# A two-layer encoder on one core: attention of the second mixer moved ahead of the third and fourth gated projections, latent vectors normalized by ScalarE out of PSUM

## The chip, the core and the metric

The kernel runs on one core of a Trainium2 chip. A core has five engines that each work through their own instruction list in order: TensorE (PE in the profile), VectorE (DVE), ScalarE (ACT), GpSimd (POOL) and SyncE (SP, which only issues DMAs here). They signal each other with semaphores. The metric is the device time of one execution in microseconds (us), median of three runs.

## What is computed

Two inputs of 256 tokens by 1024 features go through the same two-layer trunk; the kernel puts them side by side as 512 tokens. Each layer is a mixer, a residual layernorm, a convolutional feed-forward (FFN) and another residual layernorm. The change lies in the second mixer:

```
h = x @ w_in                                   # 1024 -> 256 + 128 + 32 + 512 + 512
c_q, c_kv, k_r, glu_a, glu_g = split(h)
q  = rmsnorm(c_q,  gq)  @ w_uq                 # 8 heads of 64 + 32 (the 32 are rotated)
kv = rmsnorm(c_kv, gkv) @ w_ukv                # 8 heads of 64 + 64
c  = softmax((q_nope.k_nope + q_rope.rope(k_r)) * 96**-0.5) @ v
d  = glu_a * sigmoid(glu_g)                    # the gated projection, 512 channels
d  = silu(layernorm(dwconv31(d)))              # depthwise, 31 taps along the tokens
mix = concat(c, d) @ w_out
```

All matrix products of weights are done in split fp32: each operand is a rounded high part and a low remainder, and a product is three matmuls (high by high, high by low, low by high).

## The kernel before

The kernel is written as Python loops, and a scheduler of the framework then decides the order on each engine: it lists the instructions by its own estimate of when each can start, and tile pools decide when a buffer comes free. So the order in the program text is a priority and not the final order. Pools that matter here: `actp` with 30 SBUF tiles of 4 KB per partition, `wp` with 12 weight tiles, `rawp` with 4 tiles that SyncE loads weights into, and PSUM banks in `pA` (4), `pB` (2) and `pC` (2).

`wload` (L103) loads a weight block, rounds it on ScalarE (L107, the high part) and subtracts on VectorE (L109, the low part). During the down projection of the first FFN, `KEEP` (L29) lets `glu_load` prepare all four gated weight blocks ahead, in `actp` tiles called khi and klo.

The second mixer is `odd_mixer` (L521). Its parts:

- `glu(i)` (L525), i = 0 to 3: two 128-channel projections of 24 matmuls each, sigmoid on ScalarE, product on VectorE into a padded tile `dpad`, and the start of the depthwise convolution of these 128 channels. Of the 31 taps VectorE does 21, accumulating in a PSUM bank `cacc` of `pA` (L539 and twenty of L689), and GpSimd ten: ScalarE multiplies a copy by the tap (L693, into a ring of two tiles `pr`), GpSimd adds it up (L694). L695 joins both halves.
- `cproj` (L558): the 416 latent columns, token-major, into four banks; ScalarE copies them to SBUF (L568).
- `chain` (L580): per 128 tokens the two mean squares (ScalarE L590), their inverse root (VectorE L592, GpSimd power L593), the scaling (VectorE L594), the rotation of 32 columns, and transposes on TensorE (L598, L599); ScalarE copies and rounds the result (L603, L113), VectorE makes the low part.
- `qproj` (L607) and `kvproj` (L640): queries, keys and values of all heads.
- `attend(p)` (L660) for four pairs of heads, through `attention` (L471). Per pair, sequence and head: scores in a `pB` bank, maximum on VectorE (L482), two exponentials on ScalarE (L485), reciprocal on VectorE (L488), two scalings on ScalarE (L491), four transposes `pt` into a `pC` bank (L498) and a copy on ScalarE (L500); then the product with the values, `pv`, whose result is split by ScalarE and VectorE (L113, L114).
- `conv_ln` (L697): four transposes `ct` for each 128 tokens, statistics (L157 to L162, with the power on GpSimd), normalization `cnm` (L166), transposes `cb` back, Silu and split into `mixT[4..7]`.
- `OutProj`: `first` uses `mixT[0..3]` (attention), `second` uses `mixT[4..7]` (convolution). `ToFeat` adds the residual, whose tiles GpSimd loads, multiplies (L190) and shifts (L193); two of the four residual tiles are held back until the last `ct` transpose.

The program order before is glu 0, cproj, chain, glu 1, glu 2, kvproj, qproj, glu 3, attend 0 to 3, and then the output projection with the convolution.

Of the kernel before, what the change touches and what calls it, by code (L numbers as in the profile page):

```python
# [8 lines left out]
F32 = mybir.dt.float32  # L9
F32R = mybir.dt.float32r  # L10
BF16 = mybir.dt.bfloat16
# [4 lines left out]
P = 128  # L16
# [11 lines left out]
ACUT = 832  # L28
KEEP = {4: 0, 7: 1, 10: 2, 13: 3}  # L29
EARLY = (0, 1)  # L30
# [20 lines left out]
def tile_encoder(ctx: ExitStack, tc: tile.TileContext, I, O):  # L51
# [466 lines left out]
    def glu_load(i, keep=False):  # L518
        return [wload(I["wglu"][:, i, j].rearrange("p k n -> p (k n)"), 1024, keep) for j in range(2)]

    def odd_mixer(xT):  # L521
# [3 lines left out]
        def glu(i, by_seq=False):  # L525
            pss = []
            for hi, lo in kept.pop(i, None) or glu_load(i):
                pss.append((bank(pB if i == 3 else pA, "glu"), hi, lo))
            for seqs in ((0,), (1,)) if by_seq else ((0, 1),):
                for ps, hi, lo in pss:  # L530
                    gemm_feat(ps, hi, lo, xT, seqs)
            sg = tmp([P, 512], s="sig")
            nc.scalar.activation(out=sg, in_=pss[1][0], func=AF.Sigmoid)
            d = dpad[i]
            nc.vector.tensor_tensor(out=d[:, :, 15:15 + S], in0=pss[0][0].rearrange("p (s t) -> p s t", s=2),
# [7 lines left out]

        for i in range(4):
            d = act([P, 2, S + 30], s="dpad")
            nc.gpsimd.memset(d[:, :, 0:15], 0.0)
            nc.gpsimd.memset(d[:, :, S + 15:S + 30], 0.0)
            dpad[i] = d
        acc = [act([P, 2, 2, S], s="acc") for _ in range(2)]
        acc2 = [act([P, 2, 2, S], s="acc2") for _ in range(2)]  # L550
        for a in acc + acc2:
            nc.gpsimd.memset(a[:, 0, 0, 0:1], 0.0)
# [17 lines left out]
        def apply_rope(out, src, q, nh):  # L570
            a = tmp([P, nh, 32], s="ra")
            b = tmp([P, nh, 32], s="rb")
            nc.vector.tensor_tensor(out=a, in0=src, in1=rope[:, q, 0:1, :].broadcast_to([P, nh, 32]), op=ALU.mult)
            nc.vector.tensor_tensor(out=b[:, :, 0:16], in0=src[:, :, 16:32],
                                    in1=rope[:, q, 1:2, 0:16].broadcast_to([P, nh, 16]), op=ALU.mult)
            nc.vector.tensor_tensor(out=b[:, :, 16:32], in0=src[:, :, 0:16],
                                    in1=rope[:, q, 1:2, 16:32].broadcast_to([P, nh, 16]), op=ALU.mult)
            nc.vector.tensor_tensor(out=out, in0=a, in1=b, op=ALU.add)

        def chain():  # L580
            cT = G["cT"] = [act([P, 2, T], F32R, "cT") for _ in range(3)]
            krT = G["krT"] = tmp([P, T], s="krT")
            craw = G["craw"]
            ct_ps = dn_banks()
            for t in range(NT):
                c = craw[t // 2][:, t % 2, :]
                for i, (o, w) in enumerate(((0, 256), (256, 128))):
                    ss = small(1, "ss")
                    junk = tmp([P, 256], BF16, s="junk")
                    nc.scalar.activation(out=junk[:, :w], in_=c[:, o:o + w], func=AF.Square, accum_out=ss)  # L590
                    v = small(2, "v")
                    nc.vector.tensor_scalar(out=v[:, 0:1], in0=ss, scalar1=1.0 / w, scalar2=RMS_EPS, op0=ALU.mult, op1=ALU.add)  # L592
                    nc.gpsimd.tensor_tensor(out=v[:, 1:2], in0=v[:, 0:1], in1=epsc[:, 2:3], op=ALU.pow)  # L593
                    nc.vector.tensor_scalar(out=c[:, o:o + w], in0=c[:, o:o + w], scalar1=v[:, 1:2], scalar2=None,  # L594
                                            op0=ALU.mult)
                apply_rope(c[:, None, 416:448], c[:, None, 384:416], t % 2, 1)
                for i in range(3):
                    nc.tensor.transpose(ct_ps[i][:, t * P:(t + 1) * P], c[:, i * P:(i + 1) * P], ident)  # L598
                nc.tensor.transpose(ct_ps[3][0:32, t * P:(t + 1) * P], c[:, 416:448], ident)  # L599
            for i in range(3):  # L600
                xv = tmp([P, 512], s="cv")
                g = pc("qg", i) if i < 2 else pc("kvg", 0)
                nc.scalar.activation(out=xv, in_=ct_ps[i], func=AF.Copy, scale=g)  # L603
                split(cT[i], xv)
            nc.scalar.copy(out=krT[64:96, :], in_=ct_ps[3][0:32, :])

        def qproj():  # L607
            cT = G["cT"]
            ropeT = act([P, 2, S], s="ropeT")
            after_mm(nc.gpsimd.dma_start(out=ropeT, in_=I["ropeT"]), G["start"])  # L610
            wq = [wload(I["wuq"][:, k, :], 1024) for k in range(2)]
            qT = G["qT"] = [act([P, 2, T], s="qT") for _ in range(4)]

            def qfeat(pool, c):
# [6 lines left out]
                return ps  # L621
            for r in range(2):
                ab = []
                for j in range(2):
                    ps = qfeat(pB, 4 + 2 * j + r)
                    a = tmp([P, 2, S], s="qr")
                    nc.vector.tensor_tensor(out=a, in0=ps.rearrange("p (s t) -> p s t", s=2),
                                            in1=ropeT[:, j:j + 1, :].broadcast_to([P, 2, S]), op=ALU.mult)
                    ab.append(a)
                nc.vector.tensor_tensor(out=ab[0], in0=ab[0], in1=ab[1], op=ALU.add)  # L630
                for h in range(4):
                    nc.scalar.dma_start(out=qT[2 * r + h // 2][64:96, h % 2, :],
                                        in_=ab[0][32 * h:32 * h + 32].rearrange("p s t -> p (s t)"))
                for p in (2 * r, 2 * r + 1):
                    ps = qfeat(pC, p)
                    for h in range(2):
                        nc.scalar.activation(out=qT[p][0:64, h, :], in_=ps[h * 64:h * 64 + 64, :], func=AF.Copy,
                                             scale=96 ** -0.5)

# [46 lines left out]
        for i in range(4):  # L686
# [4 lines left out]
            for j in range(32 - NPOOL, 31):  # L691
                pr = pr_ring.get()
                nc.scalar.activation(out=pr, in_=dpad[i][:, :, j:j + S], func=AF.Copy, scale=pc("cw", i * 32 + j))  # L693
                nc.gpsimd.tensor_tensor(out=a2, in0=a2, in1=pr, op=ALU.add)  # L694
            nc.vector.tensor_tensor(out=acc[i // 2][:, i % 2], in0=a, in1=a2, op=ALU.add)  # L695

        def conv_ln():  # L697
# [3 lines left out]
            for t in range(NT):  # L701
                s, q = divmod(t, 2)
                ps = bank(pA, "ct")
                for c in range(4):
                    tr = nc.tensor.transpose(ps[:, c * P:(c + 1) * P],
                                             acc[c // 2][:, c % 2, s, q * P:(q + 1) * P], ident)
                if t == NT - 1:
# [182 lines left out]
```

## Time and profile before

| | us |
|---|---|
| median of 3 runs | 1113.48 (1113.25 to 1114.97) |
| profiled execution | 1113.34 |
| its span | 1111.4 |
| TensorE busy | 1087.4 (98% of the span) |
| VectorE busy | 667.7 (60%) |
| ScalarE busy | 491.2 (44%) |
| GpSimd busy | 228.8 (21%) |

The span runs from the first to the last instruction of the profiled execution; the rest of its time lies around it. Busy times are unions of instruction durations. A matmul's duration in the trace overlaps the next one's, so that the distance from start to start is what a matmul takes. "PEclk" in the tables is the granted share of TensorE's full clock of 2.4 GHz: 1.00 is that, 0.5 is the lower level of 1.2 GHz. The second mixer takes the stretch from about 553 to 740 us.

### The profile page before, as it was taken

The page shows a single profiled execution, that of the slowest core. Times are in us where ns is not written, and L with a number is a line of the kernel's source. Part 1 is how long each engine was busy: PE and PEld are TensorE (multiplying, and loading weights), DVE is VectorE, ACT ScalarE, POOL GpSimd, SP SyncE. Part 2 cuts the span into 40 slices and gives each one's busy share as a digit, 9 for nine tenths or more (in the row PEclk, how much of TensorE's full clock was granted, in tenths as well). Part 3 has the DMA queues.
Part 4 walks back from the last instruction along what each step waited for, and adds up shares of the span by engine and source line. Part 5 has one row for each costly group of instructions (what it writes and reads, how often), then busy time and mean ns, then how long its engine had stood idle before and what let it go on. Part 6 is the DMA issues. An engine that isn't in the chain of part 4 may idle for free. (4 is left out here: it accounts for less than half of the span.)

```text
span 1111.4 us, 13663 instructions
## 1 busy us (share of the span) xinstructions
PE 1087.4 (98%) x5210; PEld 902.1 (81%) x5210; DVE 667.7 (60%) x996; ACT 491.2 (44%) x788; POOL 228.8 (21%) x230
## 2 busy tenths in 40 slices
PE   9999999999999999999998989999999999999996
PEld 7888778988888888888896757789888888888885
DVE  5378946766556566422469996567656556542227
ACT  5435645544444444311365789446444444431110
POOL 0481002100000000006465644431000000000173
PEclk9999999999999999999998979999999999999999
DMA  7942223533333323654132213234333333222501
GB/s 267 242 127 77 75 96 97 169 96 97 101 104 96 95 95 120 199 188 132 68 116 76 67 39 114 75 110 139 95 97 98 101 102 96 95 95 95 209 37 76
DMA packets 36193, 124.34 MB, mean 112 GB/s; under 512 B 4352, under 2 KB 5120, under 8 KB 36128
## 3 DMA queue, kind: packets, MB, share of 16 engines
q1 hardware_dynamic: 28224, 99.00, 28.8%
q0 software_dynamic: 6480, 22.66, 5.9%
q10 hardware_dynamic: 1424, 1.80, 0.6%
q8 instruction: 41, 0.67, 0.2%
q14 instruction: 24, 0.20, 0.1%
HBM read 114.01 MB, written 8.39 MB: 110 GB/s over the span
## 5 line engine op out<-in xcount | busy, mean ns | idle before, releaser
L96 PE MATMUL up<-xT,whi 128*128 128x512 f32 (+1 forms) x1536 | 440.2, 371 | 0.0
L109 DVE TENSOR_TENSOR wlo<-raw,whi 128x1024 fp32r<-128x1024 f32 (+1 forms) x174 | 228.9, 1317 | 290.5 <-ACT whi L107 289.2
L96 PEld LDWEIGHTS up<-xT,whi 128*128 128x128 f32 x1536 | 279.8, 188 | 49.8
L107 ACT CAST whi<-raw 128x1024 fp32r<-128x1024 f32 (+1 forms) x174 | 182.3, 1050 | 249.0 <-PE dn L96 136.1
L96 PE MATMUL up<-xT,wlo 128*128 128x512 f32 (+1 forms) x768 | 283.9, 372 | 0.0
L96 PE MATMUL dn<-whi,gT 128*128 128x512 f32 x704 | 217.6, 389 | 0.0
L96 PEld LDWEIGHTS up<-xT,wlo 128*128 128x128 f32 x768 | 144.2, 188 | 25.0
L96 PEld LDWEIGHTS dn<-whi,gT 128*128 128x128 f32 x704 | 132.0, 188 | 27.3
L96 PE MATMUL dn<-wlo,gT 128*128 128x512 f32 x352 | 137.0, 389 | 0.0
L182 POOL DMA_DIRECT2D xres<-xscr x12 | 6.5, 545 | 575.5 <-PE dn L96 574.7
L96 PEld LDWEIGHTS dn<-wlo,gT 128*128 128x128 f32 x352 | 66.1, 188 | 13.7
L113 ACT CAST gT<-cv 128x512 fp32r<-128x512 f32 x44 | 27.3, 621 | 111.8 <-DVE cv L751 111.8
L740 ACT ACTIVATE cv<-up,par 128x512 f32<-128x512 f32 x88 | 67.9, 772 | 0.0
L743 DVE SCALAR_TENSOR_TENSOR cv<-up,par,cv 128x510 f32<-128x510 f32 x88 | 65.7, 747 | 2.7
L741 DVE SCALAR_TENSOR_TENSOR cv<-up,par,cv 128x510 f32<-128x510 f32 x88 | 65.3, 742 | 0.0
L750 ACT ACTIVATE cv<-cv 128x512 f32<-128x512 f32 x44 | 27.8, 633 | 83.3 <-DVE cv L743 83.3
L689 DVE SCALAR_TENSOR_TENSOR cacc<-dpad,par,cacc 128x512 f32<-128x512 f32 x80 | 59.2, 751 | 2.0 <-DVE cacc L689 0.7
L694 POOL TENSOR_TENSOR acc<-acc,pr 128x512 f32<-128x512 f32 x36 | 49.7, 1381 | 35.4 <-ACT pr L693 33.6
L114 DVE TENSOR_TENSOR gT<-cv,gT 128x512 fp32r<-128x512 f32 x44 | 30.4, 691 | 27.5 <-ACT gT L113 27.5
L96 PE MATMUL glu<-xT,khi 128*128 128x512 f32 (+1 forms) x160 | 43.6, 360 | 2.6 <-DVE acc L695 2.6
L96 PE MATMUL op<-whi,mixT 128*128 128x512 f32 x128 | 44.2, 401 | 0.0
L96 PE MATMUL dn<-whi,mixT 128*128 128x512 f32 x128 | 42.6, 395 | 0.9 <-DVE mixT L114 0.9
(196 smaller groups left out, 1363.1 us busy)
## 6 DMA issues: line engine op xcount, KB each, us to landing
raw<-in_wup SPq DMA_DIRECT2D x88, 512.0 KB, 3.7
raw<-in_wdn SPq DMA_DIRECT2D x44, 512.0 KB, 3.5
raw<-in_wout SPq DMA_DIRECT2D x16, 512.0 KB, 3.7
xscr<-xres POOLq DMA_DIRECT2D x12, 512.0 KB, 3.8
xres<-xscr POOLq DMA_DIRECT2D x12, 512.0 KB, 4.3
raw<-in_wqk SPq DMA_DIRECT2D x8, 512.0 KB, 5.9
raw<-in_wglu SPq DMA_DIRECT2D x8, 512.0 KB, 4.0
raw<-in_wug SPq DMA_DIRECT2D x7, 512.0 KB, 3.5
```

The costliest lines, as they stand in the source:

```text
L96: last_mm[0] = nc.tensor.matmul(out=out, lhsT=lhsT, rhs=rhs, start=first, stop=last)
L107: nc.scalar.copy(out=hi[:, :n], in_=raw[:, :n])
L109: nc.vector.tensor_tensor(out=lo[:, :n], in0=raw[:, :n], in1=hi[:, :n].bitcast(F32), op=ALU.subtract)
L113: nc.scalar.copy(out=dst[:, 0, sl], in_=src)
L114: nc.vector.tensor_tensor(out=dst[:, 1, sl], in0=src, in1=dst[:, 0, sl].bitcast(F32), op=ALU.subtract)
L182: after_mm(nc.gpsimd.dma_start(out=x, in_=src[t]), after)
L689: nc.vector.scalar_tensor_tensor(out=a, in0=dpad[i][:, :, j:j + S], scalar=pc("cw", i * 32 + j), in1=a, op0=ALU.mult, op1=ALU.add)
L694: nc.gpsimd.tensor_tensor(out=a2, in0=a2, in1=pr, op=ALU.add)
L740: nc.scalar.activation(out=c, in_=pv, func=AF.Identity, scale=pc(fw, ch * 4 + 1), bias=pc(fw, ch * 4 + 3))
L741: nc.vector.scalar_tensor_tensor(out=c[:, :, 1:S], in0=pv[:, :, 0:S - 1], scalar=pc(fw, ch * 4), in1=c[:, :, 1:S], op0=ALU.mult, op1=ALU.add)
L743: nc.vector.scalar_tensor_tensor(out=c[:, :, 0:S - 1], in0=pv[:, :, 1:S], scalar=pc(fw, ch * 4 + 2), in1=c[:, :, 0:S - 1], op0=ALU.mult, o ...
L750: nc.scalar.activation(out=cg, in_=cg, func=AF.Silu)
```

## The change

The program order becomes glu 0, cproj, chain, glu 1, query weights, qproj for the first four heads, kvproj, attend 0, qproj for the other four heads, glu 2, attend 1, glu 3, attend 2, attend 3. Besides:

- only the weights of glu 0 and 1 are still prepared in the first FFN; those of glu 2 and 3 are loaded in the mixer, and their low parts are subtracted on GpSimd;
- the latent columns are no longer copied to SBUF: ScalarE squares them in PSUM, and the scaling by the inverse root is a ScalarE copy from PSUM; the four mean squares of two token blocks share one addition and one power;
- the transposed latents are rounded straight out of PSUM (ScalarE) and the remainder is made from PSUM (VectorE), without the copy between;
- `dpad` is allocated and zeroed in `glu`, and the joined convolution goes into `acc2`, so that two SBUF tiles are saved;
- Silu is written back to its PSUM bank and split from there.

```
-KEEP = {4: 0, 7: 1, 10: 2, 13: 3}
+KEEP = {4: 0, 7: 1}
...
-    def wload(src, n, keep=False):
+    def wload(src, n, keep=False, eng=None):
...
-        nc.vector.tensor_tensor(out=lo[:, :n], in0=raw[:, :n], in1=hi[:, :n].bitcast(F32), op=ALU.subtract)
+        (eng or nc.vector).tensor_tensor(out=lo[:, :n], in0=raw[:, :n], in1=hi[:, :n].bitcast(F32), op=ALU.subtract)
...
-        return [wload(I["wglu"][:, i, j].rearrange("p k n -> p (k n)"), 1024, keep) for j in range(2)]
+        return [wload(I["wglu"][:, i, j].rearrange("p k n -> p (k n)"), 1024, keep, None if keep else nc.gpsimd)
+                for j in range(2)]
...
-            craw = G["craw"] = [act([P, 2, 512], s="craw") for _ in range(2)]
-            for t in range(NT):
-                nc.scalar.copy(out=craw[t // 2][:, t % 2, 0:416], in_=psc[t][:, 0:416])
...
+                    for i, (o, w) in enumerate(((0, 256), (256, 128))):
+                        junk = tmp([P, 256], BF16, s="junk")
+                        nc.scalar.activation(out=junk[:, :w], in_=ps[:, o:o + w], func=AF.Square, scale=w ** -0.5,
+                                             accum_out=ss[:, 2 * q + i:2 * q + i + 1])
...
+                nc.vector.tensor_scalar(out=v, in0=ss, scalar1=RMS_EPS, scalar2=None, op0=ALU.add)
+                nc.gpsimd.tensor_tensor(out=v, in0=v, in1=epsc[:, 2:3].broadcast_to([P, 4]), op=ALU.pow)
+                for q in range(2):
+                    for i, (o, w) in enumerate(((0, 256), (256, 128))):
+                        nc.scalar.activation(out=c[:, q, o:o + w], in_=psc[2 * s + q][:, o:o + w], func=AF.Copy,
+                                             scale=v[:, 2 * q + i:2 * q + i + 1])
...
         chain()
         glu(1)
+        qproj_load()
+        qproj(0)
+        kvproj()
+        attend(0)
+        qproj(1)
         glu(2)
-        kvproj()
-        qproj()
+        attend(1)
         glu(3)
-        for p in range(4):
-            attend(p)
+        attend(2)
+        attend(3)
...
-            nc.vector.tensor_tensor(out=acc[i // 2][:, i % 2], in0=a, in1=a2, op=ALU.add)
+            nc.vector.tensor_tensor(out=a2, in0=a, in1=a2, op=ALU.add)
...
-                y = tmp([P, 512], s="cy")
-                nc.scalar.activation(out=y, in_=ps, func=AF.Silu, scale=pc("clg", c), bias=pc("clb", c))
-                split(mixT[4 + c], y)
+                nc.scalar.activation(out=ps, in_=ps, func=AF.Silu, scale=pc("clg", c), bias=pc("clb", c))
+                split(mixT[4 + c], ps)
```

What the scheduler makes of it stands at three places. First, TensorE where the latents are transposed (`dn_735` to `dn_738` are the transposed banks before), before the change:

```order
L599 MATMUL dn_738_4677<-ident,craw_4665 32x128
L598 MATMUL dn_735_4674<-ident,craw_4665 128x128
L598 MATMUL dn_736_4675<-ident,craw_4665 128x128
L598 MATMUL dn_737_4676<-ident,craw_4665 128x128
L96 MATMUL glu_4843<-xT_4252,khi_3887 128x512 x2
```

The same place on TensorE in the changed kernel (`dn_738` to `dn_741` are now these banks, `q` the query projection of the first four heads):

```order
L596 MATMUL dn_740_4691<-ident,craw_4660 128x128
L596 MATMUL dn_741_4692<-ident,craw_4631 32x128 x2
L596 MATMUL dn_741_4692<-ident,craw_4660 32x128 x2
L96 MATMUL q_4814<-cT_4627,whi_4779 128x512
L96 MATMUL q_4791<-cT_4627,whi_4779 128x512 x2
```

Before, the matmuls of glu 2 follow the transposes; now 24 matmuls of the query projection do, which read the transposed latents themselves, and glu 2 comes behind them.

Second, ScalarE around the sigmoid of the third gated projection. Before the change it stands ahead of all exponentials, and one table load follows the last sigmoid (that of glu 3):

```order
L533 ACTIVATE sig_5109<-glu_5060 128x512
L541 ACTIVATE acc_707_4427<-dpad_4421,par 128x512
L693 ACTIVATE pr_4432<-dpad_4421,par 128x512 x2
L485 ACT_TABLE_LOAD
L485 ACTIVATE er_5115,rs_5132<-s_5124,nmx_5130 128x256 x2
```

ScalarE in the changed kernel, between the fourth and the fifth of the 16 heads:

```order
L500 COPY PTr_4897<-pt_4952 128x512
L537 ACT_TABLE_LOAD
L537 ACTIVATE sig_5088<-glu_5036 128x512
L500 COPY PTr_4897<-pt_4967 128x512
L485 ACT_TABLE_LOAD
L485 ACTIVATE er_4892,rs_5103<-s_5095,nmx_5101 128x256
L113 CAST mixT_4900<-pv_4973 128x256
```

The sigmoids of glu 2 and glu 3 now stand between exponentials; the same pair of table loads appears again at glu 3.

Third, the tail of the mixer. TensorE before the change, in the middle of the attention of the last pair of heads (`ct` and `cb` are the transposes of the convolution's layernorm):

```order
L705 MATMUL ct_5728<-ident,acc_4424 128x128 x2
L705 MATMUL ct_5728<-ident,acc_4425 128x128 x2
L96 MATMUL s_5438<-kT_4930,qT_4976 128x256 x2
L716 MATMUL cb_5746<-ident,cnm_5698 128x128
L716 MATMUL cb_5746<-ident,cnm_5712 128x128
L716 MATMUL cb_5746<-ident,cnm_5726 128x128
L96 MATMUL pv_5387<-PTr_5119,V_785_4905 64x256 x4
L498 MATMUL pt_5410<-ident,er_5115 128x128 x4
```

TensorE in the changed kernel, behind all attention and the last matmuls of `first` (`dn_951`):

```order
L96 MATMUL dn_951_5743<-whi_5752,mixT_5356 128x512
L711 MATMUL ct_5648<-ident,acc_689_4389 128x128
L711 MATMUL ct_5662<-ident,acc_688_4388 128x128 x2
L711 MATMUL ct_5662<-ident,acc_689_4389 128x128 x2
L711 MATMUL ct_5676<-ident,acc_688_4388 128x128 x2
L711 MATMUL ct_5676<-ident,acc_689_4389 128x128 x2
L711 MATMUL ct_5690<-ident,acc_688_4388 128x128 x2
L711 MATMUL ct_5690<-ident,acc_689_4389 128x128 x2
L722 MATMUL cb_5708<-ident,cnm_5660 128x128
```

All transposes of the layernorm but three now stand in one row with no other matmul between them. GpSimd at the same place in the changed kernel:

```order
L162 TENSOR_TENSOR rstd_5657<-rstd_5657,epsc 128x1
L162 TENSOR_TENSOR rstd_5671<-rstd_5671,epsc 128x1
L190 TENSOR_TENSOR xres_5258<-xres_5258,rowg_5262 128x1024
L190 TENSOR_TENSOR xres_5260<-xres_5260,rowg_5262 128x1024
L162 TENSOR_TENSOR rstd_5685<-rstd_5685,epsc 128x1
L162 TENSOR_TENSOR rstd_5703<-rstd_5703,epsc 128x1
```

Two residual multiplications stand between the powers of the second and the third token block; before, four of them stood between those of the third and the fourth.

## Rows read from the trace of the kernel before

**Rows 1.** The page: span, and busy time of each engine.
```profile
span 1111.4 us, 13663 instructions
PE 1087.4 (98%) x5210; PEld 902.1 (81%) x5210; DVE 667.7 (60%) x996; ACT 491.2 (44%) x788; POOL 228.8 (21%) x230
```

**Rows 2.** Waits of TensorE: us in total, times, longest us.
```profile
PE s L96 <- ACT er L485: 4.4, 4, 3.0
```

**Rows 3.** Stretches: length, busy time (and instructions) of each engine, PEclk, DMA.
```profile
602.00:609.00 7.00, 4.54 (x11) 3.63 (x12) 6.84 (x11) 5.78 (x11) 1.94 (x2) 0.52 0.00 0
...
653.00:667.00 14.00, 12.63 (x40) 7.96 (x39) 13.27 (x23) 13.39 (x38) 8.88 (x7) 0.51 0.01 2
667.00:680.00 13.00, 13.00 (x82) 10.23 (x81) 10.80 (x27) 12.48 (x40) 3.37 (x7) 1.00 0.12 37
```

**Rows 4.** Timeline of TensorE: start, us, instruction, [idle before, released by].
```profile
585.42 0.38 PE L598 MATMUL dn<-ident,craw 128*128 128x128 f32 x2
...
604.46 1.22 PE L96 MATMUL glu<-xT,khi 128*128 128x512 f32 x2 [2.64 <-DVE acc L695]
...
608.47 0.77 PE L96 MATMUL glu<-xT,khi 128*128 128x512 f32 x2
...
609.31 0.62 PE L96 MATMUL glu<-xT,khi 128*128 128x512 f32 x2
...
616.13 0.61 PE L96 MATMUL glu<-xT,khi 128*128 128x512 f32 x2
...
700.65 1.19 PE L716 MATMUL cb<-ident,cnm 128*128 128x128 f32 x8
...
711.02 0.39 PE L96 MATMUL op<-whi,mixT 128*128 128x512 f32 x1
```

**Rows 5.** Timeline of ScalarE, same columns.
```profile
643.68 1.03 ACT L107 CAST whi<-raw 128x1024 fp32r<-128x1024 f32 x1
...
650.32 1.28 ACT L485 ACT_TABLE_LOAD   x1
651.62 0.47 ACT L485 ACTIVATE er<-s,nmx 128x256 f32<-128x256 f32 x1
...
652.53 0.71 ACT L693 ACTIVATE pr<-dpad,par 128x512 f32<-128x512 f32 x1
653.14 0.90 ACT L491 ACTIVATE er<-er,ri 128x256 f32<-128x256 f32 x2
...
655.45 0.58 ACT L500 COPY PTr<-pt 128x512 f32<-128x512 f32 x1
...
699.68 1.45 ACT L718 ACTIVATE cy<-cb,par 128x512 f32<-128x512 f32 x2
```

**Rows 6.** Timeline of VectorE.
```profile
584.13 1.21 DVE L109 TENSOR_TENSOR wlo<-raw,whi 128x1024 fp32r<-128x1024 f32 x1
...
674.21 1.28 DVE L157 BATCH_NORM_STATS2 st<-ct 128x6 f32<-128x512 f32 x2
...
676.83 0.78 DVE L166 TENSOR_SCALAR cnm<-ct,mv,rstd 128x512 f32<-128x512 f32 x1
...
701.42 0.42 DVE L114 TENSOR_TENSOR mixT<-pv,mixT 128x256 fp32r<-128x256 f32 x1 [3.40 <-ACT mixT L113]
701.95 5.60 DVE L114 TENSOR_TENSOR mixT<-cy,mixT 128x512 fp32r<-128x512 f32 x2
```

**Rows 7.** Timeline of GpSimd.
```profile
576.25 4.04 POOL L694 TENSOR_TENSOR acc<-acc,pr 128x512 f32<-128x512 f32 x3 [6.86 <-ACT pr L693]
...
587.24 8.41 POOL L694 TENSOR_TENSOR acc<-acc,pr 128x512 f32<-128x512 f32 x4
...
675.85 0.56 POOL L162 TENSOR_TENSOR rstd<-rstd,epsc 128x1 f32<-128x1 f32 x1 [11.44 <-DVE rstd L161]
...
687.27 9.40 POOL L190 TENSOR_TENSOR xres<-xres,rowg 128x1024 f32<-128x1024 f32 x4 [5.76 <-DMA rowg<-in_rows]
...
697.16 9.83 POOL L193 TENSOR_TENSOR xres<-xres,rowb 128x1024 f32<-128x1024 f32 x4
```

More of the change, by code (lines that the diff above doesn't have):

```diff
@@ L527, in glu @@
             for hi, lo in kept.pop(i, None) or glu_load(i):
-                pss.append((bank(pB if i == 3 else pA, "glu"), hi, lo))
+                pss.append((bank(pA, "glu"), hi, lo))
             for seqs in ((0,), (1,)) if by_seq else ((0, 1),):
@@ L565, in cproj @@
                         gemm_tok([psc[t]], xT[k], t, *wc[k // 2], [slice(o, o + 416)], k == 0, k == KC - 1)
[L566 to L578 removed]
+            G["psc"] = psc
         def chain():
@@ L582, in chain @@
             krT = G["krT"] = tmp([P, T], s="krT")
-            craw = G["craw"]
-            ct_ps = dn_banks()
[L585 to L608, printed above, removed]
+            psc = G["psc"]
+            craw = []
+            for s in range(2):
+                c = act([P, 2, 512], s="craw")
+                craw.append(c)
+                ss, v = small(4, "ss"), small(4, "v")
+                for q in range(2):
+                    ps = psc[2 * s + q]
+                    for i, (o, w) in enumerate(((0, 256), (256, 128))):
+                        junk = tmp([P, 256], BF16, s="junk")
+                        nc.scalar.activation(out=junk[:, :w], in_=ps[:, o:o + w], func=AF.Square, scale=w ** -0.5,
+                                             accum_out=ss[:, 2 * q + i:2 * q + i + 1])
+                    ra, rb = tmp([P, 32], s="ra"), tmp([P, 32], s="rb")
+                    nc.vector.tensor_tensor(out=ra, in0=ps[:, 384:416], in1=rope[:, q, 0, :], op=ALU.mult)
+                    nc.vector.tensor_tensor(out=rb[:, 0:16], in0=ps[:, 400:416], in1=rope[:, q, 1, 0:16], op=ALU.mult)
+                    nc.vector.tensor_tensor(out=rb[:, 16:32], in0=ps[:, 384:400], in1=rope[:, q, 1, 16:32],
+                                            op=ALU.mult)
+                    nc.vector.tensor_tensor(out=c[:, q, 384:416], in0=ra, in1=rb, op=ALU.add)
+                nc.vector.tensor_scalar(out=v, in0=ss, scalar1=RMS_EPS, scalar2=None, op0=ALU.add)
+                nc.gpsimd.tensor_tensor(out=v, in0=v, in1=epsc[:, 2:3].broadcast_to([P, 4]), op=ALU.pow)
+                for q in range(2):
+                    for i, (o, w) in enumerate(((0, 256), (256, 128))):
+                        nc.scalar.activation(out=c[:, q, o:o + w], in_=psc[2 * s + q][:, o:o + w], func=AF.Copy,
+                                             scale=v[:, 2 * q + i:2 * q + i + 1])
@@ new lines, in chain @@
+            ct_ps = dn_banks()
+            for i in (2, 0, 1, 3):
+                w = P if i < 3 else 32
+                for t in range(NT):
+                    nc.tensor.transpose(ct_ps[i][0:w, t * P:(t + 1) * P],
+                                        craw[t // 2][:, t % 2, i * P:i * P + w], ident)
+                if i == 3:
+                    nc.scalar.copy(out=krT[64:96, :], in_=ct_ps[3][0:32, :])
+                else:
+                    g = pc("qg", i) if i < 2 else pc("kvg", 0)
+                    nc.scalar.activation(out=cT[i][:, 0, :], in_=ct_ps[i], func=AF.Copy, scale=g)
+                    nc.vector.scalar_tensor_tensor(out=cT[i][:, 1, :], in0=ct_ps[i], scalar=g,
+                                                   in1=cT[i][:, 0, :].bitcast(F32), op0=ALU.mult, op1=ALU.subtract)
@@ L621, in qfeat @@
                 return ps
[L622 to L638, printed above, removed]
+            ab = []
+            for j in range(2):
+                ps = qfeat(pB, 4 + 2 * j + r)
+                a = tmp([P, 2, S], s="qr")
+                nc.vector.tensor_tensor(out=a, in0=ps.rearrange("p (s t) -> p s t", s=2),
+                                        in1=ropeT[:, j:j + 1, :].broadcast_to([P, 2, S]), op=ALU.mult)
+                ab.append(a)
+            nc.vector.tensor_tensor(out=ab[0], in0=ab[0], in1=ab[1], op=ALU.add)
+            for h in range(4):
+                nc.scalar.dma_start(out=qT[2 * r + h // 2][64:96, h % 2, :],
+                                    in_=ab[0][32 * h:32 * h + 32].rearrange("p s t -> p (s t)"))
+            for p in (2 * r, 2 * r + 1):
+                ps = qfeat(pC, p)
+                for h in range(2):
+                    nc.scalar.activation(out=qT[p][0:64, h, :], in_=ps[h * 64:h * 64 + 64, :], func=AF.Copy,
+                                         scale=96 ** -0.5)
         def kvproj():
```

23 lines of the change are left out of this document (12 added, 11 removed).

## The prediction

> **What bounds the kernel now.** I read the page first: TensorE is busy 1087.4 of 1111.4 us [rows 1], so all that can be won or lost lies in its few idle stretches, and in stretches where its clock is low. The list of TensorE's waits puts the largest at the start of the second mixer's attention (scores waiting for a bank that ScalarE's exponentials still read, 4.4 us in all, 3.0 in one) [rows 2]. The table of stretches shows the rest: TensorE's granted clock is 0.52 in 602 to 609 and 0.51 in 653 to 667, and 1.00 in the neighbouring stretches [rows 3]. The timeline says what the first of these cost: the latents' transposes end late, TensorE idles 2.64 us, and then nine matmuls of glu 2 take 4.01 us, from 604.46 to 608.47, while thirty later ones take 6.82, from 609.31 to 616.13 [rows 4]. So a 512-column matmul takes 0.227 us at the upper of the two levels and 0.446 here, at the lower. In the second low stretch ScalarE is busy 13.39 of 14 us, and 12.48 of 13 in the next, where the clock is back [rows 3]: attention is bound by ScalarE at either level. The program's own time is 1113.34 for a span of 1111.4, 0.14 below the median of the runs, so I add terms to 1113.34.
>
> No matmul is added or removed. The sum is made of positions on TensorE, before and after.
>
> **1. Start of the mixer.** The query weights are now loaded while glu 0 runs, and one of their remainder subtractions stands on VectorE ahead of the last residual normalization that TensorE's layernorm transposes need. It takes 1.21 [rows 6]; nothing else is behind the transposes for TensorE, so I take +1.1 (bounds 0 and 1.2).
>
> **2. Chain of the latents.** Before, the latent projections end at 585.42 and glu 2 starts at 604.46 [rows 4]: 19.0 us for 48 matmuls (10.9) and 16 short transposes (about 1.7), so 6.4 are lost. In the changed kernel the same stretch also holds 24 query matmuls (5.4): 18.0 of work. GpSimd decides when the second power can come: from 576.25 on it has eight additions at 1.35 (4.04 for three [rows 7]), three of the new subtractions and two powers of 0.56. A 128x1024 operation takes it 2.35 (9.40 for four) to 4.2 (twice 8.41 / 4, where VectorE was in its way) [rows 7]; I take 2.7. That is 576.25 + 10.8 + 8.1 + 1.1 = 596.3, when glu 1 has just ended (596.8), so the scaling on ScalarE costs TensorE about 0.5, the rounding of the first transposed latents 0.9, and the banks that the remainders hold some 0.7: 2.1 lost, end at 605.6, with 24 matmuls more done. With the slow value it would be 4.5 us later. Gain: 604.46 + 5.4 - 605.6 = 4.3, and glu 2 no longer starts at the low clock, which gives back 4.01 - 9 x 0.227 = 2.0. Together -6.3. Term 1 shifts the end to 606.7.
>
> **3. Attention.** TensorE has 55 matmuls before the last value projection is done: 606.7 + 12.5 = 619.2; with a copy and a DMA issue ScalarE begins the key copies at 620.3. From there to the last split of attention I count on ScalarE, from the order and [rows 5]: 16 heads at 0.90 for two exponentials (651.62 to 652.53), 0.80 for two scalings, 0.47 for the copy, so 34.7; 17 convolution taps at 0.61 and two first taps, 11.7; six weight roundings at 0.94, 5.6; five table loads at 1.28, 6.4; and some 26 smaller ones (copies of k, q and the attention result, two sigmoids, four DMA issues) at 0.5, 13. That is 71.4. Before, this stretch had one table load, no weight roundings in its second half, and glu 3 lay ahead of it. Besides, GpSimd gets the residual's loads, two multiplications and two shifts (2.35 to 2.46 each [rows 7]) amid the last channel group's additions, which sat 5.76 us for the broadcast row before; the ring of two tap tiles makes ScalarE wait for it. I take 3.4 (0 to 8), and 0.8 for the last product: 620.3 + 71.4 + 3.4 + 0.8 = 695.9 for the end of the last value product, which was at 700.65 [rows 4]. The gain of term 2 is thus nearly kept, not enlarged: glu 2 and 3 fill TensorE's gaps, but TensorE wasn't the engine that the gaps belonged to.
>
> Each table load takes 1.28, the instruction before it ends where it starts, and the exponential follows 0.02 after its end [rows 5]. The Trainium skill (ScalarE: Activation LUTs, What ACT_TABLE_LOAD costs) adds a drain to every switch, about 2.66 us in all. By the row the four additional switches cost 5.1, as counted above; by the page 10.6, and the whole would come out at 1130. The trace shows no such drain at the one switch that I can look at.
>
> **4. Tail.** Before, the convolution's layernorm ran beside attention, and from 700.65 TensorE went on to the rest of `first` and reached the 120 matmuls that remain at 711.02 [rows 4]: 10.4 us. Now glu 3 comes late, its convolution ends about with attention (GpSimd's additions near 700), and the `ct` transposes stand behind the last 36 matmuls of `first`. These end at 695.9 + 36 x 0.227 = 704.1. Only two `pA` banks are free for four transposed blocks, so the chain is serial: transposes 0.3; two statistics 1.3 [rows 6]; a weight remainder that stands next on VectorE 1.2 [rows 6]; two small operations and a power 0.56 [rows 7], 0.9; normalization of the first block 0.8 [rows 6], at 4.5. The second block is normalized at 5.2, the last transposes are done at 5.7; they release two residual multiplications, which stand on GpSimd ahead of the two remaining powers: 4.7 [rows 7]. Two powers 1.1, normalization 0.8: 12.4. Transposes back 0.5, Silu 0.75 [rows 5], rounding 0.7: the first matmul of `second` at 704.1 + 14.4 = 718.5, with TensorE idle for some 12 of these 14.4 us, with nothing queued that could run. Then follow the same 120 matmuls and 8 transposes (0.9). Against 711.02 that is +8.4, all terms so far included.
>
> The split of the Silu result now reads PSUM. Before, two such subtractions from SBUF took 5.60 while GpSimd's shifts ran from 697.16 for 9.83, but the subtraction that read PSUM took 0.42 at 701.42, in the same stretch [rows 6, 7]. The Trainium skill (SBUF — State Buffer, Who interferes with whom) has it so: with two inputs in SBUF VectorE waits for GpSimd's whole instruction, with one it doesn't. By that rule, and the trace agrees, the splits don't add to the 14.4; by the SBUF row each would wait up to 2.5, and the tail would be 2.5 longer.
>
> **5. Clock.** The idle 12 us are more than what preceded either fall of the clock. The nearest price is term 2's own, 2.0 for what followed an idle stretch (0 if it rises before work resumes, 6.8 if the low stretch lasts as long as the second, 13.7 us, and TensorE works through all of it). I take 2.0 for the tail, and 1.0 for the start of attention, where TensorE will again idle for a bank, but ScalarE's queue hides most of it.
>
> **Sum.** 1113.34 + 8.4 + 3.0 = 1124.7, slower by 1.0%.
>
> **Rivals.**
> - *Short tail.* GpSimd reaches the third and fourth power before the residual multiplications, and the clock is back when `second` begins. For: the multiplications wait for the last transpose. Against: the order puts them ahead of the powers, and the engine works in order. It saves 4.7 + 2.0: 1118.0.
> - *Attention is not bound by ScalarE any more.* With glu 2 and 3 in its gaps TensorE sets the pace and ScalarE's pieces overlap better than their rows. TensorE then has 70 us of work from 606.7 to the last value product and some 5 of idling, 682 instead of 695.9; the tail follows, and the convolution with it: 1124.7 - 14 = 1110.7, faster than before. For: these fillers exist. Against: ScalarE's 12.48 of 13 us at the upper clock [rows 3]. The change breaks even when the stretch from the first key copy to the last value product takes 64 us instead of 75.6.
> - *Each switch between sigmoid and exponential empties ScalarE.* The price by rows is the load's 1.28 once more for five loads, 6.4: 1131.1. Against: the two rows around the one load.
> - *It doesn't do what it says.* The order shows the projections interleaved with the attention, so I give this nothing.
>
> **How the numbers follow.** Forecast 0.63, with a range of its own of 1118 to 1131 (term 2 up to 4.5 later, term 3's ring 0 to 8, the clock 0 to 6.8); short tail 0.14; attention not bound by ScalarE 0.11; switches 0.12. The range of 1112 to 1134 leaves out most of the second rival and the ends of the last. What a measurement of this kernel can tell from no change is 0.2%, 2.2 us. Slower: 0.59 + 0.11 + 0.12 = 0.82. Within 0.2%: 0.08, from the low ends of the first two and the upper end of the third. Faster: 0.10, nearly all from the third.
>
> **What would show it.** Right: TensorE's wait before the query matmuls is under 1.5 us and the granted clock stays 1.00 there; ScalarE is busy over 90% from the first key copy to the last `pt` copy, with five table loads; the last value product ends near 696; then TensorE idles about 4 and 7 us around the `ct` transposes, the second time with GpSimd's residual multiplications running, and the clock is low when `second` starts. Wrong: the last value product before 688, or less than 6 us of idling between the end of `first` and the first matmul of `second`.

## The result and the profile after

The changed kernel takes 1133.82 us (1133.09 to 1134.42, four runs) against 1113.64 (1113.25 to 1114.97, four runs): a ratio of 1.0178 (95% interval 1.0165 to 1.0191), or 20.2 us slower. Slower was the forecast, but by 11.4 us. The profiled execution took 1133.09 with this span; the difference to the span before [rows 1] is 19.9:

```profile
span 1131.3 us, 13642 instructions
PE 1092.8 (97%) x5210; PEld 908.1 (80%) x5210; DVE 658.0 (58%) x978; ACT 496.1 (44%) x793; POOL 232.5 (21%) x226
```

The stretches of the changed kernel, with the columns of [rows 3]; the first answers to the first there:

```profile
602.00:609.00 7.00, 6.90 (x31) 5.59 (x31) 6.54 (x10) 5.35 (x9) 3.45 (x3) 1.00 0.00 0
621.00:696.00 75.00, 66.71 (x319) 49.23 (x318) 59.16 (x102) 70.69 (x166) 36.63 (x33) 0.89 0.32 99
...
710.00:718.00 8.00, 1.78 (x9) 1.25 (x8) 3.50 (x8) 0.00 (x0) 7.12 (x5) 0.50 0.02 6
718.00:726.00 8.00, 7.39 (x23) 5.68 (x22) 1.38 (x2) 2.63 (x5) 3.19 (x2) 0.51 0.00 0
726.00:755.00 29.00, 26.68 (x128) 22.01 (x126) 16.11 (x33) 13.79 (x20) 2.31 (x4) 1.00 0.35 111
757.00:763.00 6.00, 4.69 (x22) 4.50 (x22) 2.81 (x7) 2.38 (x4) 5.55 (x7) 0.50 0.19 73
```

Where the queries start the clock now stays at 1.00, and through the attention ScalarE is busy 94% of the time. Then come two stretches at 0.50: 710 to 726 around the start of the convolution's part of the output projection, and 757 to 763, where the second FFN has begun. The timeline of TensorE shows what lies ahead of them, in the columns of [rows 4]:

```profile
598.99 1.47 PE L596 MATMUL dn<-ident,craw 128*128 128x128 f32 x12
601.69 1.30 PE L96 MATMUL q<-cT,whi 128*128 128x512 f32 x3 [1.22 <-DVE cT L603]
...
607.60 0.62 PE L96 MATMUL glu<-xT,whi 128*128 128x512 f32 x2
...
693.72 1.95 PE L96 MATMUL pv<-PTr,V 128*64 128x256 f32 x16
...
703.91 0.71 PE L711 MATMUL ct<-ident,acc 128*128 128x128 f32 x5
708.86 1.94 PE L711 MATMUL ct<-ident,acc 128*128 128x128 f32 x8 [4.24 <-DVE cnm L166]
717.02 1.96 PE L722 MATMUL cb<-ident,cnm 128*128 128x128 f32 x8 [6.21 <-DVE cnm L166]
719.58 0.79 PE L96 MATMUL op<-whi,mixT 128*128 128x512 f32 x1 [0.61 <-ACT mixT L113]
...
752.20 0.48 PE L96 MATMUL dn<-whi,mixT 128*128 128x512 f32 x1
755.05 0.74 PE L96 MATMUL up<-xT,whi 128*128 128x256 f32 x4 [2.37 <-DVE xT L243]
756.31 0.46 PE L96 MATMUL up<-xT,whi 128*128 128x256 f32 x1 [0.53 <-DVE xT L245]
...
758.50 0.58 PE L96 MATMUL up<-xT,whi 128*128 128x256 f32 x1 [1.31 <-POOL xT L245]
```

All of the loss arises behind the attention, whose last value product even ends 5.0 us earlier than before (at 695.7, against 700.7), and these rows divide it. Before, the same 120 matmuls began at 711.02 [rows 4]; now the first comes at 719.58, and eight `cb` transposes (0.9) stand among them: 9.5 us. From there to the end of the last of them it is 752.68 - 719.58 = 33.1 us; before, with no wait, 711.02 to 740.04, so 29.0, and 0.9 for the transposes: 3.2 lost at the lower clock (719.6 to 725.8). TensorE then waits 2.37 + 0.53 + 1.31 = 4.2 us at the start of the FFN, where it waited for nothing before:

```profile
739.81 0.39 PE L96 MATMUL dn<-whi,mixT 128*128 128x512 f32 x1
740.04 0.64 PE L96 MATMUL up<-xT,whi 128*128 128x256 f32 x4
```

The last 3.0 of the 19.9 are a remainder, and they fall into the low stretch behind that: from the first `up` matmul to the end it took 371.4 us before and takes 376.2 now, 4.8 more, of which 1.8 are the two shorter waits.

GpSimd stood in the second of the two long waits as foreseen:

```profile
710.88 4.63 POOL L190 TENSOR_TENSOR xres<-xres,rowg 128x1024 f32<-128x1024 f32 x2 [2.48 <-PE ct L711]
715.48 1.06 POOL L162 TENSOR_TENSOR rstd<-rstd,epsc 128x1 f32<-128x1 f32 x2
716.51 4.68 POOL L193 TENSOR_TENSOR xres<-xres,rowb 128x1024 f32<-128x1024 f32 x2
```

VectorE adds the first finished piece of the projection to the residual (L197) at 719.46 before, 20.6 us ahead of the first `up` matmul, and at 739.21 after, 15.8 us ahead. The row of before, then that of after:

```profile
719.46 0.69 DVE L197 SCALAR_TENSOR_TENSOR xres<-xres,op 128x512 f32<-128x512 f32 x1 [0.71 <-PE op L96]
```

```profile
719.56 0.69 DVE L114 TENSOR_TENSOR mixT<-cb,mixT 128x512 fp32r<-128x512 f32 x1 [1.97 <-ACT mixT L113]
...
739.21 0.68 DVE L197 SCALAR_TENSOR_TENSOR xres<-xres,op 128x512 f32<-128x512 f32 x1
```

The order says why. The convolution's features (`mixT[4..7]`) come one at a time now, and whatever can run is taken: all four token blocks with the first feature block, then all with the second, and the attention part of blocks 2 and 3 between. So no token block is finished early, and behind the transposes of block 1's residual normalization (`lnT`) one matmul is left for TensorE; before, there were 15. These transposes before, with the first matmul behind them, and after:

```profile
735.74 1.03 PE L233 MATMUL lnT<-ident,xres 128*128 128x128 f32 x8
736.53 0.48 PE L96 MATMUL op<-whi,mixT 128*128 128x512 f32 x1
```

```profile
751.41 1.03 PE L233 MATMUL lnT<-ident,xres 128*128 128x128 f32 x8
752.20 0.48 PE L96 MATMUL dn<-whi,mixT 128*128 128x512 f32 x1
```

### The profile page after: what moved, and what is told of

Same layout as the page of the kernel before. It is cut to its first block, busy times and chain, and to the rows that moved or that the text cites. A ratio compares the mean times of both kernels' runs of the same rounds, so it can differ in the third digit from the quotient of the medians.

```text
span 1131.3 us, 13642 instructions
## 1 busy us (share of the span) xinstructions
PE 1092.8 (97%) x5210; PEld 908.1 (80%) x5210; DVE 658.0 (58%) x978; ACT 496.1 (44%) x793; POOL 232.5 (21%) x226
## 4 chain that ended last, share of the span: by engine, by line
PE 89%; ACT 5%; DVE 2%; issue 1%; POOL 1%; DMA 0%; POOLq 0%; ACTq 0%; DVEq 0%
PE up L96 43%; PE dn L96 28%; PE qk L96 4%; PE op L96 4%; PE glu L96 2%; PE v L96 2%; PE u L96 2%; ACT er L485 1%; PE s L96 1%; PE pv L96 1%; ACT er L491 1%; PE pt L498 1%; PE lnT L233 1%; ACT pr L699 1%; ACT whi L107 1%
## 5 line engine op out<-in xcount | busy, mean ns | idle before, releaser
L107 ACT CAST whi<-raw 128x1024 fp32r<-128x1024 f32 (+1 forms) x178 | 186.6, 1050 | 271.7 <-PE dn L96 154.2
L96 PE MATMUL qk<-xT,whi 128*128 128x512 f32 x128 | 40.6, 392 | 0.0
```

The costliest lines, as they stand in the source:

```text
L96: last_mm[0] = nc.tensor.matmul(out=out, lhsT=lhsT, rhs=rhs, start=first, stop=last)
```

## The experiments

The main theory: the loss comes from the place of glu 2 and 3 alone. They end the convolution late, its layernorm then runs with nothing beside it, and the projection that it feeds starts at the low clock and in an order that exposes the next residual norm. Rivals: ScalarE's additional work in the attention is the cost, or the new chain is. Differences are between ratios to the kernel before, times 1113.6 us; the changed kernel's is 1.0178. The pieces of code are cut to what matters, and comments in them are the document's.

**chain_alone: the new chain in the old order.** The other small edits stay; the order is written in one line here, and glu 3 gets its banks in `pB` again, as before.

```
-        glu(1); qproj_load(); qproj(0); kvproj(); attend(0); qproj(1); glu(2); attend(1); glu(3); attend(2); attend(3)
+        glu(1); glu(2); kvproj(); qproj_load(); qproj(0); qproj(1); glu(3); attend(0) ... attend(3)
-KEEP = {4: 0, 7: 1}
+KEEP = {4: 0, 7: 1, 10: 2, 13: 3}
```

> The new chain of the latents, the PSUM splits and the saved tiles stay; the program order and the four weight blocks prepared in the first FFN are those of before. Main theory (the loss comes from the late convolution, not from the chain): the chain keeps its gain of about 6 us, attention shifts left by it and the layernorm of the convolution runs beside attention again, so 1107 to 1109 us. Rival 1 (attention is paced by ScalarE and the convolution, so the chain's gain is absorbed there): 1112 to 1114. Rival 2 (the new chain and the splits out of PSUM are themselves part of the loss): over 1116.

1109.81 us, ratio 0.9961 (0.9948 to 0.9973): 4.4 faster than before, and the fastest of all. The chain's gain stays; rival 2 falls. It is less than 6 in part because the latents' first transposes come 2.2 later than before here too, at 587.6. TensorE's largest waits behind them:

```profile
PE s L96 <- ACT er L485: 3.5, 2, 3.0
PE k L96 <- DVE cT L603: 1.8, 1, 1.8
```

**glus_ahead: only glu 2 and 3 go back ahead of the attention.**

```
         kvproj()
+        glu(2)
+        glu(3)
         attend(0)
         qproj(1)
-        glu(2)
         attend(1)
-        glu(3)
```

> The changed kernel, with glu 2 and glu 3 moved ahead of the first attention block; queries, keys and values still come before them, and the second half of the queries still comes behind the first attention block. Main theory (the loss comes from the place of glu 3 alone): the convolution ends while attention runs, TensorE has no idle stretch around the ct transposes, the rest of the output projection and the second FFN begin at the full clock, and of the 20 us some 20 to 24 go, so 1110 to 1114. Rival (attention is paced by ScalarE, so that whatever is put ahead of it moves its end): the last value product comes 10 us later than in the changed kernel and eats most of it, 1120 to 1125.

Ratio 1.0001 (0.9991 to 1.0010): all of the loss is gone. The rival had the fact right and not its price: the last value product ends at 705.4, ten us later than in the changed kernel, but the `ct` transposes lie amid the attention and nothing waits behind it. Against chain_alone this kernel is still 4.5 us slower. It differs from it in the order of queries, keys and values and in the two weight blocks that are loaded in the mixer; which of the two costs that, no run shows.

```profile
704.29 1.08 PE L96 MATMUL pv<-PTr,V 128*64 128x256 f32 x6
707.48 1.03 PE L722 MATMUL cb<-ident,cnm 128*128 128x128 f32 x8
...
741.70 0.76 PE L96 MATMUL up<-xT,whi 128*128 128x256 f32 x5
```

**order_alone: the new order with the old chain.** The edit puts the old functions cproj and chain back into the changed kernel.

> The changed kernel with the chain of the latents as before (a copy of the latent columns to SBUF, four additions and powers, a copy of the transposed latents ahead of their rounding). Main theory (the new order delays the convolution, the new chain is a gain of its own, and the two add up): the queries wait longer for the latents and all behind them is late by what the chain alone gave, 4.4 us, so 1133.8 + 4.4 = about 1138. Rival (the end is set by the convolution, whose place the chain doesn't move): 1134.

Ratio 1.0280 (1.0265 to 1.0295), 31 us slower than before: the chain is worth 11.4 in this order, not 4.4, and my expectation was 7 us short. In the old order glu 2 covers part of the latents' wait; here the queries stand directly behind it and all else behind them. TensorE starts them at 610.23, against 601.69 above (1.4 of these 8.5 us lie ahead of the latents already):

```profile
594.31 0.44 PE L595 MATMUL dn<-ident,craw 128*128 128x128 f32 x2 [2.79 <-DVE craw L591]
...
610.23 1.20 PE L96 MATMUL q<-cT,whi 128*128 128x512 f32 x4 [3.50 <-ACT cT L113]
```

**affine_late: the two residual multiplications behind the powers.**

```
-                if t == NT - 1:
-                    sink.res.affine([u for u in range(NT) if u not in EARLY], tr)
...
-                    nc.tensor.transpose(ps[:, t * P:(t + 1) * P], ns[t][:, c * P:(c + 1) * P], ident)
+                    tr = nc.tensor.transpose(ps[:, t * P:(t + 1) * P], ns[t][:, c * P:(c + 1) * P], ident)
+                if c == 0:
+                    sink.res.affine([u for u in range(NT) if u not in EARLY], tr)
```

> The changed kernel, with the two held back residual multiplications tied behind the first cb transposes instead of the last ct transpose, so that on GpSimd they stand behind the last powers. Main theory (they keep the two powers from 710.9 to 715.5): the second idle stretch of TensorE shrinks from 6.2 to about 1.6 us, the first matmul of the convolution part comes at 715, and the time is 1133.8 - 4.6 = about 1129, or 1127.5 if the low clock ends as early. Rival (the normalization on VectorE waits for something else, or the multiplications now hold up the splits): 1132 to 1134.

Ratio 1.0138 (1.0123 to 1.0154): 4.5 saved, as expected. The wait of 6.21 is 1.91 + 0.79 now, 3.5 less and not the 4.6 that were expected of it, and from the `ct` transposes to the end the profiled execution saves 3.6; the times alone can't tell 3.6 from 4.5. GpSimd's multiplications run from 716.52 on, behind the last power.

```profile
710.45 1.94 PE L711 MATMUL ct<-ident,acc 128*128 128x128 f32 x8 [4.24 <-DVE cnm L166]
714.30 0.88 PE L720 MATMUL cb<-ident,cnm 128*128 128x128 f32 x3 [1.91 <-DVE mv L159]
715.96 1.33 PE L720 MATMUL cb<-ident,cnm 128*128 128x128 f32 x5 [0.79 <-DVE cnm L166]
```

**blocks_in_turn: token blocks 0 and 1 finished first.**

```
             for t in range(NT):
+                if t == 2 and mid is not None:
+                    mid(last_mm[0])      # first(0, (2, 3)), tied behind this matmul
```

> The changed kernel, but in the output projection the 24 matmuls that finish the attention part of token blocks 2 and 3 are tied behind the last matmul of blocks 0 and 1, so that these two blocks are finished first. Main theory (TensorE's idle 4.2 us at the start of the second FFN and the low clock behind it, 2.8 us, come from blocks finished too late, because the convolution's features arrive one by one and all blocks are worked on together): both go, 1133.8 - 7.0 = about 1127, and TensorE has no wait over 0.3 us before the first matmul of the FFN. Rival (the residual normalization is late because the whole tail is late, whatever the order): TensorE waits for the third and fourth feature block instead, 1132 to 1134.

Ratio 1.0127 (1.0113 to 1.0141): 5.7 saved of the 7. `up` starts without a wait, and from its first matmul to the end it takes 371.4 us, as before the change; the first transposes of the residual norm wait 1.82 instead, which is what is missing.

```profile
743.13 1.06 PE L237 MATMUL lnT<-ident,xres 128*128 128x128 f32 x8 [1.82 <-DVE xres L217]
...
755.85 0.52 PE L98 MATMUL up<-xT,whi 128*128 128x256 f32 x3
```

**zeros_in_tail: matmuls of zeros in TensorE's two waits.**

```
+                if t in FILL:            # {1: 24, 3: 40}
+                    for _ in range(FILL[t]):
+                        mm(op.ps[0][0][:, 0:256], warm[:, 0:P], warm, False, False)
+                        after_mm(last_mm[0], tr)
```

> The changed kernel with 24 and 40 additional matmuls of zeros (128x256, bf16, added into an accumulator that they don't change) behind the second and the fourth ct transposes, where TensorE idled 4.2 and 6.2 us. Main theory (the idle gaps are what brings the clock down, and the low clock costs 3 us when the rest of the output projection begins): the granted clock stays at 1.00 from 700 to 745, the first matmul of the convolution part stands where it was, near 719.6, and the time is 1133.8 - 3 = about 1130.7. Rival (the clock falls for another reason, or the 6 us of low clock hide waits for the features that come back): 1133 to 1135.

Ratio 1.0154 (1.0140 to 1.0168), 2.7 saved, which looks like the theory. The profile does not bear it out: the clock is 1.00 through the waits, but then falls and is low over the same matmuls as before, and from the `ct` transposes to the end the profiled execution saves 0.5. So the low clock's cost isn't isolated by this run, and the 2.7 are not explained.

```profile
710.00:718.00 8.00, 5.42 (x46) 4.29 (x44) 2.51 (x7) 1.01 (x2) 8.00 (x6) 1.00 0.01 3
718.00:726.00 8.00, 7.03 (x20) 5.63 (x21) 1.29 (x2) 2.06 (x4) 2.15 (x1) 0.57 0.00 0
```

**tail_mended: the last three together**, with 24 and 12 matmuls of zeros.

> The changed kernel with the three edits of blocks_in_turn, zeros_in_tail (24 and 12 matmuls of zeros, since the second gap is shorter) and affine_late together. Theory 1 (the three costs lie one after the other in time and are separate): the savings add, 5.7 + 2.7 + 4.5 = 12.9 of the 20.2 us, a ratio to the kernel before of 1.006; TensorE's first wait of 4.2 us at the ct transposes stays, and with it most of what is left. Theory 2 (a shorter idle stretch already saves most of the low clock, or the zeros delay the transposes): 10 to 11 saved, 1.008 to 1.009.

Ratio 1.0093 (1.0076 to 1.0110): 9.5 saved, below both theories, though each of the four intervals is 3 to 4 us wide. Within the profiles, from the `ct` transposes to the end, the three alone save 3.6, 5.4 and 0.5, and together 10.6: there they add, to within 1.1. TensorE's waits of 4.2 and 6.2 are down to 1.6 and 1.3, of which the zeros hide a part without saving it; the wait for the first feature block, 0.6 in the changed kernel, is 1.6 here, and the low clock behind it ends after 2.9 us and not after 6.2. The other half of the 20.2 us stays: the chain still stands alone behind `first`, 11.9 us instead of 15.7.

```profile
PE lnT L238 <- DVE xres L218: 1.8, 1, 1.8
PE ct L718 <- DVE cnm L171: 1.6, 1, 1.6
PE op L99 <- ACT mixT L118: 1.6, 1, 1.6
PE cb L731 <- DVE cnm L171: 1.3, 1, 1.3
```

**sigmoid_by_exp and sigmoid_by_tanh: no table loads amid the attention.** For glu 2 and 3 alone:

```
-            nc.scalar.activation(out=sg, in_=pss[1][0], func=AF.Sigmoid)
+            nc.scalar.activation(out=sg, in_=pss[1][0], func=AF.Exp, scale=-1.0)
+            nc.vector.tensor_scalar(out=sg, in0=sg, scalar1=1.0, scalar2=None, op0=ALU.add)
+            nc.vector.reciprocal(out=sg, in_=sg)
```
```
+            nc.scalar.activation(out=sg, in_=pss[1][0], func=AF.Tanh, scale=0.5)
+            nc.vector.tensor_scalar(out=sg, in0=sg, scalar1=1.0, scalar2=0.5, op0=ALU.add, op1=ALU.mult)
```

> The changed kernel, with the sigmoid of glu 2 and 3 made from the exponential (ScalarE) and an addition and a reciprocal (VectorE), so that four table loads amid the attention go. Main theory (attention is paced by ScalarE, each load is worth its 1.28 us and no more): the last value product ends 5.1 us earlier, near 690.6, the convolution's additions, which follow ScalarE's tap copies, end near 696 to 700, and the time falls by 4 to 5, to 1129 to 1130. Rival 1 (the convolution's own end on GpSimd and VectorE sets the tail): the value product is early and the ct transposes are not, 1132 to 1134. Rival 2 (every switch costs a drain as well, another 1.3 us): 1124.

> The changed kernel with the sigmoid of glu 2 and 3 made from tanh, which the exponential's table holds too: 0.5 + 0.5 tanh(x/2), one more VectorE instruction of 0.62 us each instead of the exponential version's 0.62 and 3.34. Four table loads amid the attention go as before. Theory 1 (attention is paced by ScalarE, as predicted; the exponential version was late only because its two reciprocals of 3.34 us held up VectorE): the last value product ends 4 to 5 us earlier, near 691. The tail then begins when the convolution ends; VectorE's taps, which ended at 700.8, take over as the bound, so that of the 4.5 only some 2 to 3.5 reach the end: 1130.3 to 1132. Theory 2 (attention is paced by VectorE already): the value product moves by less than 1.5 us and the time stays at 1133 to 1134.5.

Both 1.0174 (1.0161 to 1.0187 and to 1.0188): nothing is gained. The exponential version adds a VectorE reciprocal of 3.34 us to each of the two, the tanh version nothing of that size: one table load is left of five, and ScalarE works 66.41 of the 76.7 us from the key copies to the last value product instead of 70.39 of 74.7.

```profile
643.08 3.34 DVE L542 RECIPROCAL sig<-sig 128x512 f32<-128x512 f32 x1
```

```profile
622.50:699.20 76.70, 67.14 (x326) 48.59 (x325) 59.58 (x103) 66.41 (x163) 38.56 (x34) 0.93 0.30 97
```

So 4 us less work on ScalarE made the stretch 2 us longer. Theory 1 falls. Theory 2 isn't shown by it: VectorE has idle time too (59.58 of 76.7). The order on all engines changed with the edit, and TensorE now waits 3.55 in one place for a split of the attention's result on VectorE. What paces the attention stays open. And since the convolution ends at 700.8 in all three kernels, an earlier value product could have brought the `ct` transposes forward from 703.9 to 700.8 at the most.

**exp_glus_mid, tanh_glus_mid, chain_tanh: attempts at a faster version.** New chain, four kept weight blocks; the first two have glu 2 ahead of the first attention block and glu 3 behind it, the third is chain_alone with tanh.

> A version meant to beat both: the new chain, queries of the first four heads, keys and values, then glu 2, the first attention block, the other queries, glu 3, and the rest of attention; all four gated weight blocks prepared in the first FFN as before; the sigmoid of glu 2 and 3 by exponential and reciprocal, so that no table is switched in the attention. Main theory: the convolution ends inside attention as before, glu 3 fills TensorE's gaps at the start of attention, and attention is shorter by the table loads and the weight roundings that ScalarE no longer has in it: 1102 to 1107. Rival (the convolution of the last group still ends behind attention): 1110 to 1118.

> As exp_glus_mid (new chain, queries first, glu 2 ahead of the first attention block, glu 3 behind it, four prepared weight blocks), with all sigmoids made from tanh in place of the exponential and reciprocal. Theory 1 (exp_glus_mid was late because of the reciprocals on VectorE, 6.7 us): 1118 - 6 = about 1112, or down to 1107 if the convolution no longer holds anything up. Theory 2 (attention's end is set by the amount of work put ahead of and into it, on whichever engine): the last value product stays at 705 to 708, and the time at 1116 to 1118.

> The new chain in the old program order (as in chain_alone), and all four sigmoids made from tanh. Main theory: in this order no sigmoid stands between exponentials, so only small things on ScalarE and VectorE move; within 1 us of chain_alone's 1109.8, 0.4% below before. Rival: the scheduler's different order around the glus costs or gains more than 2 us.

Ratios 1.0042 (1.0030 to 1.0054), 1.0082 (1.0068 to 1.0095) and 0.9973 (0.9963 to 0.9982). Both guesses at glu 3 in the middle were wrong; without the reciprocals it even got slower, so theory 1 falls. Theory 2 has the last value product 5 us too late (it ends at 699.8) and the time some 5 us too short. The profiles show where tanh_glus_mid loses: it reaches the first `up` matmul at 743.3, exp_glus_mid at 744.3, but from there to the end it takes 375.9 us against 371.4. TensorE waits 4.0 us at the start of the FFN, with the clock at 0.51 behind that, as in the changed kernel; in exp_glus_mid it does not wait there. Why the order comes out so in the one and not in the other no run shows. chain_tanh is 1.3 us behind chain_alone, less than the two intervals can tell apart.

## Why the prediction was right, and where it was too small

The direction was right, and so, in the main, was the path: every sign that the prediction named as showing it right came, with waits of 4.2 and 6.2 us where it had about 4 and 7. The number was not. 1133.82 lies above the forecast's own range of 1118 to 1131, and inside the wider one of 1112 to 1134 by 0.2 us only. The room above 1131 was there for the rival of the switches, which no run here bears out: that the range held is luck.

- **Term 1** (+1.1): 2.2, and from another instruction. The latents' first transposes come at 587.64, against 585.42 [rows 4]. Two subtractions of the latent weights (2.15), not one of the query weights, stand ahead of the residual normalization now.
- **Term 2** (-6.3): right. The wait ahead of the queries is 1.22, the clock there 1.00, and glu 2 begins at 607.60, forecast 606.7.
- **Term 3** (695.9): the number was right (the last value product ends at 695.7), the reason only half. Five table loads of 1.28 stand there, and ScalarE is busy 70.4 us (94%), forecast 71.4. But the ring of tap tiles cost 0.7 instead of 3.4, and 3.6 of other waits of ScalarE, which the sum doesn't have, made up for it: so near a hit is in part luck. And taking 4 us of work from ScalarE did not shorten the stretch. A queue that is full is not yet the one that paces.
- **Term 4** (chain of 14.4 behind `first`): right but for 1.3: it begins at 703.9, forecast 704.1, and takes 719.58 - 703.91 = 15.7. affine_late shows the multiplications' share, 3.5 of TensorE's wait (4.5 by the times) for the 4.7 that I put on them. The rival of a short tail falls with it.
- **Term 5** (clock, 3.0): 3.2 at the start of `second`, where I had put 2.0. The 1.0 for the attention doesn't show: the last value product ended where term 3 alone had put it.
- **What failed** is a sentence in term 4: "Then follow the same 120 matmuls and 8 transposes". They are the same, but not in the same order, and I ended the sum with them: nothing was put on the start of the second FFN. What follows cost 4.2 us of waiting and 3.0 at the low clock, 7.2 of the 8.4 by which the profiled execution was later than forecast. blocks_in_turn shows the cause. The order of the changed kernel had it to be read: one matmul behind the second `lnT`, where before there were 15.
- **Switches.** The Trainium skill (ScalarE: Activation LUTs, What ACT_TABLE_LOAD costs) adds a drain to each. Here the instruction before ends where the load begins, and the next begins 0.01 us after it; no drain shows:

```profile
638.35 0.56 ACT L500 COPY PTr<-pt 128x512 f32<-128x512 f32 x1
638.93 1.28 ACT L537 ACT_TABLE_LOAD   x1
640.22 0.60 ACT L537 ACTIVATE sig<-glu 128x512 f32<-128x512 f32 x1
```

- **Splits out of PSUM.** They took 0.69 at 719.56, while GpSimd's shifts ran from 716.51 to 721.2, so they were not held up. The Trainium skill (SBUF — State Buffer, Who interferes with whom) has it so, and the trace agrees.

## What to carry to other kernels

When work is moved so that a dependent chain comes last, price the chain, and then read in the new order what stands behind it: inputs that arrived one by one made the scheduler spread the remaining work over all outputs here, and the next stage's norm had nothing left to hide under. Fillers help only if they aren't the start of a longer chain: glu 3 filled TensorE's gaps, and 38 us of convolution behind it became the end of the stage. A faster chain was worth more where it stood directly ahead of its users than where other work lay between (11.4 against 4.4 us here).

## What was not expected of the hardware

VectorE's reciprocal of 128x512 fp32 took 3.34 us, where its addition of two inputs on that shape took 0.69. And the same start of the mixer, with the same waits of 1.9 and 0.4 us, was followed by some 3.4 us at the clock 0.50 in the profiles of affine_late, blocks_in_turn and tail_mended, and by none in those of the changed kernel and zeros_in_tail; all behind it was 1.3 to 1.6 us later. The stretch in the changed kernel, then in affine_late, 53 matmuls against 40:

```profile
563.00:571.00 8.00, 7.61 (x53) 7.34 (x52) 5.02 (x13) 3.48 (x8) 2.97 (x5) 1.00 0.57 232
```

```profile
563.00:571.00 8.00, 7.61 (x40) 7.23 (x39) 5.02 (x13) 3.49 (x8) 2.97 (x5) 0.79 0.59 230
```

Differences of that size between two single profiles say nothing of an edit.
